# Low parts of the weights formed on GpSimd in a two-layer diffusion backbone

## The chip, the cores and the metric

One core of a Trainium2 chip runs the whole program in one launch. The metric is the time of one execution on the device, in microseconds (us); smaller is better. The engines are named as in the rows of the profile: PE is TensorE (matmuls; PEld is its weight load), DVE is VectorE, ACT is ScalarE, POOL is GpSimd, SP is SyncE, whose queue issues nearly all transfers.

## What is computed

Two layers over 2048 latent tokens and 256 context tokens of width 1024. The even layer is a Conformer convolution (31 taps) beside a Fourier mixing, the odd layer a short gated convolution beside windowed attention. Cut to its frame:

```
def _even_mix(h, w_in, a_conv_w, a_conv_b, a_ln_g, a_ln_b, a_pw_w, a_pw_b, b_fw, w_out):
    a_val, a_glu, a_gate, b_val, b_gate = _split(h @ w_in, ...)
    u = a_val * jax.nn.sigmoid(a_glu)
    u = jax.nn.silu(_layernorm(_dwconv(u, a_conv_w) + a_conv_b, a_ln_g, a_ln_b))
    y_a = (u @ a_pw_w + a_pw_b) * jax.nn.silu(a_gate)
    y_b = _fourier_mix(b_val, b_fw) * jax.nn.silu(b_gate)
    return jnp.concatenate([y_a, y_b], axis=-1) @ w_out

# reference(), per layer
x_new = x + gt * _even_mix(_pre(x, e_norm[i], sh, sc), *args)
...
x_new = x + gt * _odd_out(cb, cc, cx, cg, att, ag, o_c_conv_w[i], o_w_out[i])
return _rmsnorm(x, final_norm)
```

All of it is in float32.

## The kernel before

A product in float32 is made of three products of a shorter format, fp32r. Each operand is split into a high part, the value rounded to fp32r, and a low part, the value less its high part, rounded too; `gemm` (lines 117 to 124) multiplies high by high (L122), high weight by low activation (L123) and low weight by high activation (L124). `split` (lines 92 to 95) forms both parts: a copy on ScalarE writes the high part (L94), a subtraction on VectorE the low part (L95).

Tokens lie along the free dimension in chunks: four of 512 latent tokens (0 to 3) and one of 256 context tokens (4). The weights come as blocks of 128 output channels. `wblock` loads a block of 1024x128 in two halves; `wload` (lines 102 to 108) does one half: a transfer on SyncE's queue into a staging tile `wst` of 128x512 (three buffers), then `split` into the tiles `wh` and `wl` (three buffers of a whole block each). The pointwise weights of the convolution go the same way under the names `pwst`, `pwh` and `pwl`, from `conv0`. There are 148 blocks and so 296 halves, and 20 halves of pointwise weights. Activations, attention probabilities and FFT intermediates go through `split` too; those calls are others than that of `wload`.

The gemms are the main line, stage by stage: `in0` (input projection of the even layer) for chunks 0, 1 and 4, `in0` for chunks 2 and 3, `wout0` (its output projection) for chunks 4 and 0, then 1, `in1` (input projection of the odd layer) for 4, 0 and 1, `wout0` for 2 and 3, `in1` for 2 and 3, `wout1` for all. A group of two or three blocks is loaded, then used for each chunk in turn. The gemms fill three PSUM buffers (`pmm`), and VectorE and ScalarE evict them.

Beside it runs a second line, `mixers` and then `attention`, woven in by `merge` with a ratio for each stage. `mixers` is: `taps` for chunks 0 and 1, `conv0(0)`, `taps` for 4, `conv0(4)`, then the four FFT groups with the modulation sums of `mod_rows` between them, then `conv0(1)`, `taps` for 2 and 3, `conv0(2)`, `conv0(3)`. A tap (L419) is one multiply-add over half a chunk or a whole one on VectorE, whose two tensor inputs (the gated signal or its differences, and the running sum) lie in SBUF; the first tap of a channel group (L454) has one tensor input. `conv0` is the layer norm, SiLU and pointwise product of the convolution. The buffers of taps and `conv0` and those of the FFT lie in the same place, one after the other; attention's come after them there.

The order of the instructions on each engine is not written out. A planner takes instructions as they become ready in its own model of the chip, by priority: the code order sets it, `high_priority` shifts it (taps are put back by 100), and it hands out the buffers. Each engine then works its list in order and waits by semaphores where an input is not there. On GpSimd that list holds 28 small memsets of tile edges, the memset of one 128x512 tile done twice at the start, and 44 issues of transfers of the DFT tables (L661), three buffers deep; the transfers of all else are on SyncE's list.

Of the kernel before, what the change touches and what calls it, by code (L numbers as in the profile page):

```python
# [9 lines left out]
F32 = mybir.dt.float32  # L10
# [3 lines left out]
ALU = mybir.AluOpType  # L14
# [60 lines left out]
class Kernel:  # L75
# [26 lines left out]
    def wload(self, src, w, k, kt=KT):  # L102

        pre = "w" if kt == KT else "pw"
        pool, bufs = (self.wp, 3) if kt == KT else (self.vp, 1)
        st = self.tl(pool, [P, 4, P], F32, pre + "st", bufs=bufs)
        self.nc.sync.dma_start(st, src[:, k : k + 4])
        self.split(st, w[0][:, k : k + 4], w[1][:, k : k + 4])

    def wblock(self, src, kt=KT):  # L110

# [1270 lines left out]
```

## Time and profile before

| | before |
|---|---|
| median of three runs | 1931.48 us |
| lowest and highest | 1931.21 and 1932.12 us |
| the profiled execution | 1931.29 us |
| its span (first to last instruction) | 1929.5 us |
| PE busy | 1850.1 us, 96% |
| DVE busy | 1471.3 us, 76% |
| ACT busy | 917.6 us, 48% |
| POOL busy | 35.6 us, 2% |

Busy times are of one profiled execution. Matmuls overlap, and their ends are modelled, so a busy PE is not PE at its peak. Instructions of one engine overlap a little as well: their durations add up to more than the distance of their starts. An L with a number is a line of the kernel before. A releaser is what ended an engine's idle time, inferred from semaphores.

### The profile page before, as it was taken

How to read it: one execution, taken by the hardware profiler on the slowest of the kernel's cores; microseconds unless marked ns; L12 is line 12 of the kernel's file. 1: busy time of each engine (PE TensorE's matmuls, PEld its weight loads, DVE VectorE, ACT ScalarE, POOL GpSimd, SP SyncE). 2: the span in 40 equal slices, each digit the busy share in tenths (PEclk: the TensorE clock that was granted, in tenths of full speed). 3: DMA queues.
4: the chain of work that ended last, by engine and by line, in shares of the span. 5: the costliest groups of instructions: out<-in, count | busy, mean ns of one | idle time of the engine just before them, and what ended most of it. 6: DMA issues, size and time to landing. Idle time of an engine off the chain costs nothing.

```text
span 1929.5 us, 26744 instructions
## 1 busy us (share of the span) xinstructions
PE 1850.1 (96%) x9140; PEld 1498.5 (78%) x9140; DVE 1471.3 (76%) x3234; ACT 917.6 (48%) x1630; POOL 35.6 (2%) x78
## 2 busy tenths in 40 slices
PE   6899999989999999999999999999999999999997
PEld 2688878867777887888877877777787777888887
DVE  4799999879986989999644567688745556577866
ACT  5732242523223534422332666565665655576543
POOL 0000000011011000000000000000000000000000
PEclk9999999999999999999999999999999999999998
DMA  8433242778677487774135246567633232354754
GB/s 308 139 112 114 88 134 89 239 227 257 231 228 208 152 281 238 217 202 144 59 120 161 92 140 212 159 191 200 167 112 110 83 98 74 96 178 146 227 179 159
DMA packets 216600, 316.87 MB, mean 164 GB/s; under 512 B 22928, under 2 KB 102288, under 8 KB 215440
## 3 DMA queue, kind: packets, MB, share of 16 engines
q1 hardware_dynamic: 204496, 299.96, 49.6%
q0 software_dynamic: 11968, 15.21, 3.2%
q8 instruction: 72, 1.18, 0.3%
q14 instruction: 64, 0.52, 0.1%
HBM read 240.90 MB, written 74.19 MB: 163 GB/s over the span
## 4 chain that ended last, share of the span: by engine, by line
PE 68%; DVE 11%; issue 10%; DMA 8%; ACT 2%; SPq 0%; POOL 0%; DVEq 0%; POOLq 0%; ACTq 0%
PE mm L123 18%; PE mm L124 18%; PE mm L122 18%; DVE z L419 5%; PE pv L930 4%; PE pt L995 4%; PE s L930 4%; DMA et<-in_e_tab 2%; DMA xk<-gbd 1%; DMA act<-in_e_w_mod 1%; DMA yd<-pev 1%; DVE wl L95 1%; DMA wst<-in_e_w_out 1%; DMA pwst<-in_e_a_pw_w 1%; ACT S L980 1%
## 5 line engine op out<-in xcount | busy, mean ns | idle before, releaser
L122 PE MATMUL mm<-act,wh 128*128 128x512 f32 (+1 forms) x2288 | 861.7, 378 | 11.8 <-ACT act L211 10.0
L123 PE MATMUL mm<-act,wh 128*128 128x512 f32 (+1 forms) x2288 | 863.8, 378 | 0.3 <-DVE act L95 0.2
L124 PE MATMUL mm<-act,wl 128*128 128x512 f32 (+1 forms) x2288 | 860.6, 377 | 0.9 <-DVE wl L95 0.9
L122 PEld LDWEIGHTS mm<-act,wh 128*128 128x128 f32 x2288 | 431.9, 189 | 84.4 <-ACT act L211 11.5
L123 PEld LDWEIGHTS mm<-act,wh 128*128 128x128 f32 x2288 | 432.3, 189 | 71.2 <-issue 2.6
L124 PEld LDWEIGHTS mm<-act,wl 128*128 128x128 f32 x2288 | 432.4, 189 | 69.5 <-issue 2.4
L94 ACT CAST wh<-wst 128x512 fp32r<-128x512 f32 x296 | 176.3, 620 | 283.9 <-PE mm L123 217.7
L95 DVE TENSOR_TENSOR wl<-wst,wh 128x512 fp32r<-128x512 f32 x296 | 197.7, 686 | 55.2 <-ACT wh L94 53.2
L419 DVE SCALAR_TENSOR_TENSOR z<-d,e_a_conv_w,z 128x504 f32<-128x504 f32 (+2 forms) x372 | 206.4, 611 | 0.2
L95 DVE TENSOR_TENSOR pl<-pt,ph 128x512 fp32r<-128x512 f32 x156 | 102.0, 686 | 54.0 <-ACT ph L94 53.1
L94 ACT CAST ph<-pt 128x512 fp32r<-128x512 f32 x156 | 85.4, 590 | 99.9 <-PE pt L995 92.2
L980 ACT ACTIVATE S<-S,nb 128x640 f32<-128x640 f32 (+1 forms) x128 | 103.0, 806 | 57.2 <-DVE nb L976 57.1
L995 PE MATMUL pt<-ident,S 128*128 128x128 f32 x624 | 121.6, 274 | 2.3 <-ACT S L987 1.4
L995 PEld LDWEIGHTS pt<-ident,S 128*128 128x128 f32 x624 | 80.2, 140 | 40.6 <-ACT S L987 15.1
L419 DVE SCALAR_TENSOR_TENSOR z<-ut,ws,z 128x504 f32<-128x504 f32 (+2 forms) x180 | 101.6, 610 | 0.1
L987 ACT ACTIVATE S<-S,sm 128x640 f32<-128x640 f32 (+1 forms) x128 | 94.0, 806 | 9.9 <-DVE sm L985 9.8
L960 DVE CUSTOM_DVE_ANT_0 S<-s,mask 128x384 f32<-128x384 f32 (+1 forms) x128 | 68.6, 536 | 16.4 <-PE s L930 9.9
L211 ACT ACTIVATE act<-nu,mod 128x512 fp32r<-128x512 f32 (+1 forms) x80 | 52.5, 678 | 42.2 <-DVE nu L210 41.9
L930 PE MATMUL s<-kw,qs 128*128 128x384 f32 (+1 forms) x256 | 67.3, 343 | 1.6 <-DMA kw<-kd 1.3
L212 DVE SCALAR_TENSOR_TENSOR act<-nu,mod,act 128x512 fp32r<-128x512 f32 (+1 forms) x80 | 54.7, 694 | 6.5 <-ACT act L211 6.1
L969 DVE TENSOR_SCALAR_CACHE_REDUCE S<-s 128x256 f32<-128x256 f32 x128 | 53.5, 419 | 6.0 <-PE s L930 5.5
L930 PEld LDWEIGHTS s<-kw,qs 128*128 128x128 f32 x256 | 44.0, 188 | 15.8 <-DVE mx L960 5.3
(252 smaller groups left out, 2034.7 us busy)
## 6 DMA issues: line engine op xcount, KB each, us to landing
wst<-in_o_w_in SPq DMA_DIRECT2D x104, 256.0 KB, 3.2
wst<-in_e_w_in SPq DMA_DIRECT2D x80, 256.0 KB, 3.3
wst<-in_o_w_out SPq DMA_DIRECT2D x64, 256.0 KB, 3.3
mw<-in_o_w_mod SPq DMA_DIRECT2D x48, 256.0 KB, 3.6
wst<-in_e_w_out SPq DMA_DIRECT2D x48, 256.0 KB, 3.8
et<-in_e_tab POOLq DMA_DIRECT2D x28, 384.0 KB, 4.4
kw<-kd SPq DMA_DIRECT2D x28, 384.0 KB, 3.5
act<-in_e_w_mod SPq DMA_DIRECT2D x32, 256.0 KB, 5.4
```

The source lines that it names most:

```text
L94: nc.scalar.copy(hi, src)
L95: nc.vector.tensor_tensor(lo, src, hi.bitcast(F32), ALU.subtract)
L122: mm(ps, hi[:, k, :], act.hi[k], start=k == 0, stop=False)
L123: mm(ps, hi[:, k, :], act.lo[k], start=False, stop=False)
L124: mm(ps, lo[:, k, :], act.hi[k], start=False, stop=k == kt - 1)
L212: nc.vector.scalar_tensor_tensor(act.lo[k], u, sh[:, k, v : v + 1], act.hi[k].bitcast(F32), ALU.add, ALU.subtract)
L419: nc.vector.scalar_tensor_tensor(*a)
L930: nc.tensor.matmul(*a, **kw)
L960: nc.vector.tensor_tensor_reduce(s[:, :nw], ps[:, :nw], self.mask[:, m0 : m0 + nw], op0=ALU.add, op1=ALU.max, scale=1.0, scalar=-3.0e38, a ...
L980: nc.scalar.activation(S[h], S[h], AF.Exp, bias=nb4[:, h : h + 1], scale=SM_SCALE, accum_out=sm[:, h : h + 1],)
L987: nc.scalar.activation(S[h], S[h], AF.Copy, scale=sm[:, h : h + 1])
L995: nc.tensor.transpose(pt[:, h * P : (h + 1) * P], S[h][:, i * P : (i + 1) * P], self.ident)
```

## The change

`wload` no longer calls `split`. It writes the high part with the same copy on ScalarE and forms the low part with the same subtraction, issued on GpSimd. All other calls of `split` stay on VectorE.

```diff
--- before.py
+++ after.py
@@ -105,7 +105,9 @@
         pool, bufs = (self.wp, 3) if kt == KT else (self.vp, 1)
         st = self.tl(pool, [P, 4, P], F32, pre + "st", bufs=bufs)
         self.nc.sync.dma_start(st, src[:, k : k + 4])
-        self.split(st, w[0][:, k : k + 4], w[1][:, k : k + 4])
+        hi, lo = (x[:, k : k + 4] for x in w)
+        self.nc.scalar.copy(hi, st)
+        self.nc.gpsimd.tensor_tensor(lo, st, hi.bitcast(F32), ALU.subtract)
 
     def wblock(self, src, kt=KT):
 
```

## Rows read from the trace of the kernel before

**Rows 1.** The page, part 1: busy us, share of the span, instructions.

```profile
PE 1850.1 (96%) x9140; PEld 1498.5 (78%) x9140; DVE 1471.3 (76%) x3234; ACT 917.6 (48%) x1630; POOL 35.6 (2%) x78
```

**Rows 2.** By stage: length; busy of PE, PEld, DVE, ACT, POOL; clock; DMA.

```profile
0.00:96.00 96.00, 71.58 (x313) 44.18 (x314) 60.61 (x120) 62.02 (x96) 1.35 (x8) 0.96 0.66 224
96.00:365.00 269.00, 263.30 (x1356) 222.62 (x1357) 259.00 (x532) 93.53 (x157) 1.11 (x10) 1.00 0.39 121
365.00:620.00 255.00, 234.11 (x1194) 193.16 (x1192) 209.09 (x507) 71.18 (x138) 31.85 (x47) 0.98 0.77 234
620.00:936.00 316.00, 309.18 (x1446) 255.71 (x1447) 303.38 (x509) 126.84 (x215) 0.25 (x3) 0.99 0.63 193
936.00:1320.00 384.00, 373.89 (x1754) 295.98 (x1752) 242.05 (x573) 202.23 (x360) 0.69 (x7) 1.00 0.48 150
```

**Rows 3.** What PE waited for, whole span: us in total, times, longest.

```profile
PE aux L638 <- DMA et<-in_e_tab: 10.8, 15, 2.4
...
PE aux L630 <- DVE fG L618: 5.8, 1, 5.8
...
PE mm L124 <- DVE wl L95: 0.9, 3, 0.4
```

**Rows 4.** Chain that ended last, by line, 96 to 365, 620 to 936.

```profile
by line: PE mm L124 21.7%; PE mm L122 21.5%; PE mm L123 21.4%; DVE z L419 15.9%; DMA pwst<-in_e_a_pw_w 3.2%; DMA wst<-in_e_w_in 2.5%; issue 1.8%; DVE wl L95 1.3%; DVE lt L95 1.0%; DVE pwl L95 1.0%; ACT z L533 0.8%; DVE pev L553 0.7%; ACT pw
...
by line: PE mm L123 19.2%; PE mm L122 19.1%; PE mm L124 19.0%; DVE z L419 18.5%; DMA wst<-in_e_w_out 4.1%; issue 3.0%; DVE wl L95 2.3%; DMA xk<-gbd 1.4%; DMA ga<-gad 1.3%; DMA xk<-yd 1.3%; ACT wh L94 1.0%; DVE act L95 1.0%; PE aux L194 1.0%
```

**Rows 5.** Groups of DVE, 96 to 365: count, busy us, mean ns, idle before.

```profile
L419 DVE SCALAR_TENSOR_TENSOR z<-d,e_a_conv_w,z 128x504 f32<-128x504 f32 x124 | 83.4, 735 | 0.1
...
L95 DVE TENSOR_TENSOR wl<-wst,wh 128x512 fp32r<-128x512 f32 x38 | 25.8, 684 | 2.7 <-ACT wh L94 2.7
...
L95 DVE TENSOR_TENSOR pwl<-pwst,pwh 128x512 fp32r<-128x512 f32 x8 | 5.5, 691 | 2.5 <-ACT pwh L94 2.5
```

**Rows 6.** Timeline of DVE at 223.5: start us, us, instruction.

```profile
223.50 0.68 DVE L95 TENSOR_TENSOR wl<-wst,wh 128x512 fp32r<-128x512 f32 x1
224.11 0.73 DVE L419 SCALAR_TENSOR_TENSOR z<-d,e_a_conv_w,z 128x504 f32<-128x504 f32 x1
```

**Rows 7.** Groups of POOL, whole span.

```profile
L661 POOL DMA_DIRECT2D et<-in_e_tab x44 | 31.6, 719 | 269.6 <-PE aux L638 179.7 <-DMA bvd<-ev 77.1 <-DMA et<-in_e_tab 9.0
...
L234 POOL MEMSET ev<- 128x512 f32 x2 | 1.0, 525 | 0.3 <-POOLq L1377 0.3
L438 POOL MEMSET ut<- 128x15 f32 x8 | 0.9, 112 | 123.0 <-DVE z L419 114.9 <-DVE lt L493 8.1
```

**Rows 8.** Timeline at 154, DVE and POOL.

```profile
154.27 0.54 DVE L454 TENSOR_SCALAR z<-ut,ws,e_a_conv_b 128x504 f32<-128x504 f32 x1
154.46 0.39 POOL L436 MEMSET ut<- 128x15 f32 x1 [43.12 <-DMA wst<-in_e_w_in]
```

**Rows 9.** Timeline at 197, DVE and POOL.

```profile
196.87 1.39 DVE L419 SCALAR_TENSOR_TENSOR z<-ut,ws,z 128x504 f32<-128x504 f32 x2
...
197.71 0.11 POOL L436 MEMSET ut<- 128x15 f32 x1 [42.85 <-DVE z L419]
```

**Rows 10.** Instructions with wl by stage: length; PE, PEld, DVE busy us (count).

```profile
365.00:620.00 255.00, 98.37 (x248) 47.24 (x248) 20.05 (x30) 0.98 0.77 234
620.00:936.00 316.00, 170.25 (x458) 86.53 (x458) 42.52 (x64) 0.99 0.63 193
```

**Rows 11.** What POOL waited for, 365 to 620.

```profile
POOL et L661 <- PE aux L638: 179.7, 21, 54.4
```

**Rows 12.** What the queue of SP waited for, 560 to 700.

```profile
SPq L107 <- DVE wl L95: 8.1, 8, 3.7
SPq L711 <- DVE lt L95: 5.1, 1, 5.1
```

**Rows 13.** Line 393 (evictions of in0's last kind), 600 to 700.

```profile
L393 ACT ACTIVATE ev<-mm x8: 581/598/602, 615.9 to 662.7; 128x512 f32<-128x512 f32 x8
```

**Rows 14.** Timeline of SP at 1047.

```profile
1047.89 0.47 SPq L315 DMA_DIRECT2D kw<-kd  x1
```

## The prediction

> **What bounds the kernel now.** I read the page first, then one table of engine time by stage, then what TensorE waited for, then the chain of waits in the two stages in which VectorE is full, and last the rows of GpSimd. The page [rows 1] shows TensorE busy for 1850.1 of 1929.5 us and GpSimd for 35.6. So at most 79.4 us can be had by feeding TensorE better. The table by stage [rows 2] says where VectorE matters: from 96 to 365 us it is busy for 259.0 of 269.0 us, from 620 to 936 for 303.4 of 316.0, while TensorE has 5.7 and 6.8 us idle there. From 365 to 620 VectorE has 45.9 us idle, from 936 to 1320 142.0. The list of TensorE's waits [rows 3] is to be read for what is not in it: the instruction that the change moves, the forming of wl, is waited for 3 times, 0.9 us in all. Larger are its waits for the DFT tables (10.8 us in 15 waits) and for one of the FFT's additions on VectorE (5.8 us). The chain of waits [rows 4] gives VectorE's convolution taps (L419) 15.9% of the stage 96 to 365 and 18.5% of the stage 620 to 936, and wl 1.3% and 2.3%: 0.013 x 269 + 0.023 x 316 = 10.8 us. So TensorE bounds, and VectorE is level with it in two stages: its taps fill every gap, and what follows them (the layer norm of the convolution, then the FFT in the place of its buffers) starts when they end.
>
> **What is removed.** All 296 wl and the 20 pwl leave VectorE; line 108 is their only source. One takes 684 ns [rows 5], and the next instruction starts 0.61 us after it (223.50 to 224.11) [rows 6], so a stage loses 0.61 us of VectorE for each: 46 of them from 96 to 365 (38 + 8) [rows 5] are 28.1 us. Of that little was on the path: TensorE's own waits for wl, 0.9 us [rows 3], are the direct gain, and I take 1 us.
>
> **What is added, on GpSimd.** No row of before shows an elementwise operation with two inputs on this engine. Its nearest row is the memset of the same 128x512 tile, one pass of writes: 525 ns [rows 7]. Lower bound of the price: VectorE's 0.68 us [rows 5]. Upper bound: three such passes one behind the other, two reads and a write, 1.58 us. I take two passes, 1.05 us, since that row is of the same engine, and the write can run beside the reads. 296 + 20 of them are 332 us of GpSimd, 17% of the span, so the engine is not filled.
>
> **Do the two engines get in each other's way?** Two pairs of rows bear on it. The memset of 15 columns takes 112 ns as a rule [rows 7], and it does so beside a tap [rows 9]. But at 154.46 it took 0.39 us, beside the one kind of tap instruction with a single tensor input (L454, 154.27 to 154.81), and ended with it, 0.04 us later [rows 8]. So there are VectorE instructions that hold GpSimd off until they are done. Whether a GpSimd instruction that reads two tiles holds off a tap, which also reads two tiles of SBUF, no row shows. The bounds: each wl on GpSimd gives VectorE back 0.61 us and blocks it for nothing (net -0.61), or it gives back 0.61 and blocks VectorE for its whole duration (net 1.58 - 0.61 = +0.97 at the dear price). I take a full block at 1.05 us, net +0.44 us, because the only instructions that show an interaction show a wait to the end of the other, and because a tap and the moved instruction are alike in reading two tiles of SBUF, where the memset reads none.
>
> The Trainium skill, "SBUF — State Buffer", section "SBUF: two separate sides", has a rule that speaks against this change: VectorE and GpSimd share a pair of ports as an exclusive lock, a VectorE operation with two SBUF inputs collides only with a GpSimd operation that reads SBUF, and the one that starts first holds the pair for its whole instruction. The two pairs of memset rows (which only write) agree with that as far as they go; by the rule the net is +0.44 us, and without the lock -0.61. The Trainium skill, "GPSIMD Engine Reference", section "Elementwise — side-by-side cycle accounting", gives two-input fp32 work on GpSimd 1.96 times VectorE's duration; as an estimate that is 1.34 us here, a net of +0.73, and the sum below would be about 1959 us.
>
> **The sum by stage.** 0 to 96 us: 8 wl, in a stage that leaves VectorE 35.4 us idle [rows 2]; nothing. 96 to 365: 46 x 0.44 = 20.2 us more of VectorE; its 10.0 us of idle time take the first part, and 10.2 us come out at the end, where the last of conv0(4) makes room for the FFT's tiles. 365 to 620: 31 x 0.44 = 13.6 us (30 wl [rows 10] and one pwl) fit into 45.9 us of idle time; nothing more, but nothing comes back either, since the FFT's chain is one of transfers and waits. Its end gates conv0(1), and conv0(1) gates wout0: the queue of SyncE stands for 5.1 us at the first loads of wout0's activations, behind conv0(1)'s last low part [rows 12]. The last eviction of in0 is at 662.7 us [rows 13], so TensorE has no other matmuls left there, and I take the 10.2 us as idle time of TensorE. 620 to 936: 68 x 0.44 = 29.9 us (64 wl [rows 10] and 4 pwl), 12.6 of them into idle time, 17.3 us pushed on. They delay the last taps, and the first loads of attention, which follow them at 1047.89 us [rows 14]. Taken at nothing: matmuls of in1 stand ready for TensorE, and VectorE has 142.0 us of idle time in the next stage [rows 2]; if that cover is gone it costs up to 17.3. After 936: VectorE is busy for 63% of the stage up to 1320, and less is asked of it; nothing.
>
> **Queues.** The cast on ScalarE, the staging load and its slot stay, but the slot is now released by GpSimd: SyncE's queue waited 8.1 us for wl in 8 waits between 560 and 700 us [rows 12], with the loads of activations and the stores behind it. A wl that comes 0.4 to 0.5 us later adds about 4 us to these waits, half of it seen by TensorE: +2 us (0 to 11, the whole of wl's share of the chain again). On GpSimd's own queue the wl now stand among the 44 issues of DFT tables, 0.72 us each [rows 7]. An issue behind a wl is late by up to 1.05 us; GpSimd is busy with wl for 30 x 1.05 = 32 of 255 us there, so some 5 or 6 of 44 issues meet one, half of it each: +2 us on the 15 waits for tables (0 to 16, if all 15 meet one). The other way round, a wl behind an issue that waits for TensorE is a rival below.
>
> Sum: -1 + 10.2 + 2 + 2 = +13.2 us. The profiled execution took 1931.3 us (span 1929.5), 0.2 below the median of 1931.48; 1931.3 + 13.2 + 0.2 = 1944.7, so **1945 us**.
>
> **Rivals.**
> A, absorbed. VectorE's taps are filler; if the 10.2 us at 365 are taken back inside the 20.9 us that TensorE idles from 365 to 620 [rows 2], only the queues are left: +0 to +4 us, 1933 us. For it: TensorE has enough matmuls of in0 through the whole of that stage. Against it: the loads that wait for conv0(1) [rows 12].
> B, faster: the two engines do not collide, or only briefly. It decides at a block of under 0.61 us for each wl. Then VectorE is 28.1 us ahead at 365, the FFT starts sooner, and TensorE's waits for VectorE fall: 5.8 us at the FFT's additions, 0.9 at wl [rows 3], and about 5.1 at wout0's loads [rows 12]: 11.8 us at most. I take 8: 1923 us. For it: memsets ran undisturbed beside taps [rows 9]. Against it: the one that did not [rows 8].
> C, much slower: GpSimd's queue is one line. The issues of DFT tables stood there for 179.7 us in 21 waits for TensorE [rows 11]. A wl behind such an issue is late although its inputs are ready, and matmuls of in0 stop for it. At 1 us for each of the 21, with the forecast's 13.2 and the 17.3 us of the stage up to 936 also coming through: 1931.5 + 13.2 + 21 + 17.3 = 1983 us; one of the two alone gives 1962 to 1966. It decides where the planned order, which places a wl where its inputs are due, is off by more than the time by which wl are early.
>
> **How the numbers follow.** Forecast (1936 to 1958) 0.42, A 0.20, B 0.20, C 0.18. Within 0.2%, about what a measurement of this kernel can tell from no change, is 1927.6 to 1935.4. B lies below it, of A nearly all is within it, forecast and C are above. Faster 0.22, same 0.19, slower 0.59. The range takes in A, most of B and the two single cases of C, and the dear price of the forecast (46 x 0.97 - 10.0 = 34.6 in place of 10.2, 1969 us): 1920 to 1972.
>
> **What would show it.** Right: a wl on GpSimd of 1.0 to 1.3 us; taps beside one that read 1 us longer or start later; VectorE's busy time down by less than the 191 us that 316 x 0.61 gives, or up; the FFT's first table later than now; a wait of TensorE at 660 to 700 us. Taps of unchanged 735 ns [rows 5] beside wl would make B right and the forecast wrong. An unchanged end of conv0(4) with the same time would say A; matmuls of in0 that wait for wl on GpSimd, between 365 and 620 us, would say C. The step that I trust least is the 10.2 us that goes from VectorE's overrun to TensorE.

## The result: 6.5% slower, and the profile after

The changed kernel takes 2057.8 us (median; 2055.3 to 2059.1) where the kernel before takes 1931.6 beside it: a ratio of 1.0646, with a 95% interval of 1.0629 to 1.0664. The change costs 126 us. The forecast was 1945 us, with a range of 1920 to 1972: the sign was right and the time lies 86 us above the range.

The rows of the changed kernel have its own line numbers, two higher behind `wload`: L421 is the tap, L110 GpSimd's low part. Each experiment's rows likewise have those of its kernel. The first part of the page (busy us, share of the span, instructions) answers [rows 1]; under it, from its second part, TensorE's busy tenths in 40 slices of the span:

```profile
PE 1884.1 (92%) x9140; PEld 1516.2 (74%) x9140; DVE 1458.2 (71%) x2918; ACT 922.6 (45%) x1633; POOL 529.1 (26%) x394
...
PE   7799898888989988979899999998999999999997
```

GpSimd now works for 529.1 us instead of 35.6. VectorE has 316 instructions less, but its busy time fell only from 1471.3 to 1458.2 us, by 13.1, where 316 x 0.61 would be 193. TensorE does the same 9140 matmuls in 1884.1 us instead of 1850.1. So the 123.7 us by which the span grew (2053.2 against 1929.5) are 89.7 us more of idle TensorE and 34.0 us more of TensorE at work, at a lower granted clock (0.97 in the mean, before 0.99). The digits show where: the sevens and eights lie in the first half.

The stages, cut as in [rows 2] (length; busy us and instructions of PE, PEld, DVE, ACT, POOL; granted clock; DMA):

```profile
96.00:365.00 269.00, 238.30 (x1161) 198.74 (x1160) 252.74 (x467) 79.46 (x133) 89.62 (x47) 0.95 0.31 98
365.00:620.00 255.00, 219.26 (x1103) 182.06 (x1101) 200.09 (x430) 68.23 (x126) 76.59 (x69) 0.95 0.68 208
620.00:936.00 316.00, 276.86 (x1306) 226.47 (x1307) 279.56 (x412) 118.19 (x208) 96.29 (x71) 0.94 0.62 189
936.00:1320.00 384.00, 367.14 (x1661) 292.99 (x1659) 208.68 (x428) 163.88 (x283) 85.87 (x66) 0.98 0.44 134
```

In 96 to 365 us TensorE is busy for 238.3 us where it was 263.3, at a clock of 0.95 where it was 1.00; the next two stages lose 14.9 and 32.3 us of TensorE's work. From 936 to 1320 us the loss is 6.8.

TensorE's waits (us in all, times, longest), which answer [rows 3]:

```profile
PE bg L522 <- DVE lt L518: 18.7, 2, 9.9
PE aux L196 <- DVE rb L188: 17.0, 3, 8.3
...
PE mm L126 <- POOL wl L110: 12.3, 4, 9.9
PE aux L640 <- DMA et<-in_e_tab: 9.4, 14, 1.8
...
PE aux L196 <- DVE nt L188: 7.9, 2, 4.3
PE aux L632 <- DVE fG L620: 7.8, 1, 7.8
...
PE bg L126 <- POOL pwl L110: 6.4, 8, 1.1
```

The waits for the DFT tables did not grow (9.4 us in 14, before 10.8 in 15). Much longer are the waits for VectorE's sums: lt, which the layer norm's mean needs, and rb and nt, which hold squares and their sums for the norms. In the kernel before they were:

```profile
PE aux L194 <- DVE rb L186: 3.2, 1, 3.2
...
PE bg L520 <- DVE lt L516: 1.8, 2, 1.0
```

New is a wait of 9.9 us for a low part on GpSimd. Summed over the whole list by the engine that ended the wait, TensorE waited 101.6 us for VectorE and 21.7 for GpSimd; before, 30.6 for VectorE and nothing for GpSimd. The groups of VectorE from 96 to 365 us (count, busy us, mean ns), which answer [rows 5]:

```profile
L421 DVE SCALAR_TENSOR_TENSOR z<-d,e_a_conv_w,z 128x504 f32<-128x504 f32 x124 | 87.8, 779 | 0.1
...
L456 DVE TENSOR_SCALAR z<-ut,ws,e_a_conv_b 128x504 f32<-128x504 f32 x3 | 3.5, 1183 | 0.0
```

Those of GpSimd over the whole span, which answer [rows 7]:

```profile
L110 POOL TENSOR_TENSOR wl<-wst,wh 128x512 fp32r<-128x512 f32 x296 | 465.7, 1589 | 1203.0 <-ACT wh L109 1142.8 <-DMA mw<-in_o_w_mod 23.8 <-DMA wst<-in_e_w_in 8.6
...
L110 POOL TENSOR_TENSOR pwl<-pwst,pwh 128x512 fp32r<-128x512 f32 x20 | 29.1, 1457 | 111.6 <-ACT pwh L109 108.1 <-DMA ga<-gad 3.5
```

And the view of that one tile (duration in ns: least, median, greatest):

```profile
L110 POOL TENSOR_TENSOR wl<-wst,wh x296: 1257/1302/18003, 26.3 to 2026.7; 128x512 fp32r<-128x512 f32 x148
```

The 124 taps are still 735 ns as a rule; their mean is 779 because six last 1.4 to 1.8 us. Even the operation with one tensor input (L456), 535 ns in the kernel before, has a mean of 1183. A low part on GpSimd has a mean of 1589 ns, but half of them take up to 1302, and one 18003. That one in the timeline (start us, us), which joins instructions that follow each other:

```profile
213.41 21.38 POOL L110 TENSOR_TENSOR wl<-wst,wh 128x512 fp32r<-128x512 f32 x3 [5.71 <-ACT wh L109]
```

And VectorE's timeline where it ends:

```profile
226.38 2.70 DVE L421 SCALAR_TENSOR_TENSOR z<-d,e_a_conv_w,z 128x504 f32<-128x504 f32 x4
229.00 0.69 DVE L452 TENSOR_TENSOR d<-ut 128x519 f32<-128x519 f32 x1
...
230.22 1.74 DVE L421 SCALAR_TENSOR_TENSOR z<-ut,ws,z 128x504 f32<-128x504 f32 x1
231.88 1.77 DVE L517 TENSOR_TENSOR lt<-lt,z 128x512 f32<-128x512 f32 x1
```

From 213.41 us the subtraction on GpSimd stands beside 24 taps of unchanged 0.74 us (the DVE rows before 229), and gets through only at 230, beside the next row's first tap, which lasts 1.74 us. The GpSimd row runs over three low parts in a row, to 234.8; the two behind the first take 1.72 and 1.66 us and lengthen the next VectorE instructions to 1.77. So there are two effects: GpSimd can be **held off** by VectorE, and when it gets in it **blocks** VectorE for about 1 us.

The issues of DFT tables on GpSimd (first and last start), before and after, as the view of that tile has them:

```profile
L661 POOL DMA_DIRECT2D et<-in_e_tab x44: 716/716/832, 370.8 to 594.2; - x44
...
L663 POOL DMA_DIRECT2D et<-in_e_tab x44: 713/713/859, 401.5 to 650.4; - x44
```

And the last evictions of the first projections, which answer [rows 13]:

```profile
L395 ACT ACTIVATE ev<-mm x8: 580/598/601, 672.0 to 724.7; 128x512 f32<-128x512 f32 x8
```

The FFT's first table is issued at 401.5 us instead of 370.8. The last of those evictions starts at 724.7 us instead of 662.7. GpSimd's issues waited 88.1 us for TensorE over the whole span, less than the 179.7 of [rows 11].

### The profile page after: what moved, and what is told of

Same layout as the page of the kernel before. It is cut to its first block, busy times and chain, and to the rows that moved or that the text cites. A ratio compares the mean times of both kernels' runs of the same rounds, so it can differ in the third digit from the quotient of the medians.

```text
span 2053.2 us, 26873 instructions
## 1 busy us (share of the span) xinstructions
PE 1884.1 (92%) x9140; PEld 1516.2 (74%) x9140; DVE 1458.2 (71%) x2918; ACT 922.6 (45%) x1633; POOL 529.1 (26%) x394
## 5 line engine op out<-in xcount | busy, mean ns | idle before, releaser
L126 PE MATMUL mm<-act,wl 128*128 128x512 f32 (+1 forms) x2288 | 872.3, 382 | 12.4 <-POOL wl L110 12.3
L110 POOL TENSOR_TENSOR wl<-wst,wh 128x512 fp32r<-128x512 f32 x296 | 465.7, 1589 | 1203.0 <-ACT wh L109 1142.8
L124 PEld LDWEIGHTS mm<-act,wh 128*128 128x128 f32 x2288 | 437.0, 191 | 93.8 <-ACT act L213 10.5
L126 PEld LDWEIGHTS mm<-act,wl 128*128 128x128 f32 x2288 | 437.7, 191 | 85.0 <-POOL wl L110 14.5
L125 PEld LDWEIGHTS mm<-act,wh 128*128 128x128 f32 x2288 | 437.7, 191 | 79.2 <-DVE act L95 5.7
L421 DVE SCALAR_TENSOR_TENSOR z<-d,e_a_conv_w,z 128x504 f32<-128x504 f32 (+2 forms) x372 | 236.7, 693 | 0.2
L421 DVE SCALAR_TENSOR_TENSOR z<-ut,ws,z 128x504 f32<-128x504 f32 (+2 forms) x180 | 128.1, 747 | 0.7
L188 DVE TENSOR_TENSOR rb<-rb,nt 128x512 f32<-128x512 f32 (+1 forms) x70 | 56.5, 808 | 27.0 <-ACT nt L187 26.6
L214 DVE SCALAR_TENSOR_TENSOR act<-nu,mod,act 128x512 fp32r<-128x512 f32 (+1 forms) x80 | 61.1, 774 | 8.4 <-ACT act L213 7.9
L866 DVE TENSOR_TENSOR m<-mm,ev 128x512 f32<-128x512 f32 x16 | 11.0, 690 | 77.8 <-PE mm L126 74.6
```

The costliest lines, as they stand in the source:

```text
L110: self.nc.gpsimd.tensor_tensor(lo, st, hi.bitcast(F32), ALU.subtract)
L124: mm(ps, hi[:, k, :], act.hi[k], start=k == 0, stop=False)
L125: mm(ps, hi[:, k, :], act.lo[k], start=False, stop=False)
L126: mm(ps, lo[:, k, :], act.hi[k], start=False, stop=k == kt - 1)
L421: nc.vector.scalar_tensor_tensor(*a)
```

## The experiments

Theory 1: GpSimd's operation on two SBUF tiles and VectorE's operations on SBUF tiles exclude each other, and this costs the time. Theory 2: the change made the planner lay another order of instructions, and the order is worse. Theory 3: only GpSimd's longer time and the low parts' lateness cost. Theory 4: any pass of GpSimd over SBUF costs VectorE its time.

### Is it GpSimd's reading? (e8, e9, e12)

> The changed kernel, in which GpSimd sets each low part to zero instead of forming it: the same tiles are written by the same engine and read by TensorE, in nearly the instruction order of the change, but GpSimd reads nothing. Theory 1 (GpSimd's reads of two tiles beside VectorE's reads of two tiles): near the kernel before, 1925 to 1945 us. Theory 2 (the changed order of instructions costs): stays at 2040 to 2070 us. Theory 4 (any pass of GpSimd over SBUF costs VectorE its time, here 0.53 us instead of 1.26): 1970 to 2000 us.

```
-        self.nc.gpsimd.tensor_tensor(lo, st, hi.bitcast(F32), ALU.subtract)
+        self.nc.gpsimd.memset(lo.bitcast(F32), 0.0)
```

Measured: 1920.7 us, 0.9943 of the kernel before (0.9920 to 0.9965), 4 us below the range of theory 1. Of TensorE's 9140 matmuls in the order of the trace, a comparison line by line finds 192 that stand elsewhere than in the changed kernel; for the kernel before it finds 737. So with nearly the order of the change, with GpSimd writing the same tiles and TensorE waiting for them, the loss is gone, and 10 us beside it. Theories 2 and 4 fall. The run takes away two things at once, GpSimd's reading and more than half of its time (0.53 us instead of 1.26); the next two take them apart. A memset on GpSimd added to the kernel before (e5) gave no time: with its tile the others no longer fitted in SBUF (11 kb a partition needed, 10.3 left). The write-only kernel also gives each VectorE instruction of the change its undisturbed twin. Its page:

```profile
PE 1847.5 (96%) x9140; PEld 1499.1 (78%) x9140; DVE 1292.8 (68%) x2918; ACT 921.6 (48%) x1633; POOL 191.3 (10%) x394
```

An addition of two SBUF tiles (L188) among its groups:

```profile
L188 DVE TENSOR_TENSOR rb<-rb,nt 128x512 f32<-128x512 f32 x49 | 33.7, 688 | 12.2 <-ACT nt L187 11.7
```

The same group in the changed kernel, and one that reads PSUM, the masked scores:

```profile
L962 DVE CUSTOM_DVE_ANT_0 S<-s,mask 128x384 f32<-128x384 f32 x112 | 61.9, 553 | 12.1 <-PE s L932 9.2 <-PE pt L997 1.7
...
L188 DVE TENSOR_TENSOR rb<-rb,nt 128x512 f32<-128x512 f32 x49 | 45.1, 920 | 21.0 <-ACT nt L187 20.7
```

VectorE's busy time is 1292.8 us here and 1458.2 there, for the same 2918 instructions: 165 us are waiting for GpSimd, written down as work. Taken instruction by instruction (each one's duration less the median of its form here) it is 164.9 us, and 187 instructions are more than 0.3 us longer, by 0.89 us on average. By stretch of the span, all instructions together grew by 33.5 us from 96 to 400 us (35 of the 187), by 18.6 up to 655 (22), by 49.3 up to 1000 (54) by 58.2 behind it (70), and by 5.2 before 96 us (6). The additions at L188 go from 688 to 920 ns. The masked scores, which read PSUM, keep their 553 ns.

> The changed kernel in which GpSimd writes half of the staged weight as the low part (a one-input operation of 128x512) instead of the difference: nearly the same order of instructions, the same tiles written and waited for, but one tile read instead of two. In the second microkernel three one-input operations lengthened a row of 36 taps by 0.67 us, three two-input ones by 3.0 us. Theory 1 (two reads are what blocks): 1925 to 1960 us. Rival (any read of GpSimd's blocks VectorE): 2020 to 2060 us.

```
-        self.nc.gpsimd.tensor_tensor(lo, st, hi.bitcast(F32), ALU.subtract)
+        self.nc.gpsimd.tensor_scalar(lo, st, 0.5, None, ALU.mult)
```

Measured: 1985.3 us, 1.0285 (1.0259 to 1.0311), between what the two said. One read costs too, if less: VectorE's instructions are 37.8 us longer in all, 90 of them by 0.37 us on average, though GpSimd itself is slower at it (mean 1718 ns, instead of 1589). Neither "only two reads" nor "any read as much" holds, and GpSimd's longer time by itself does not make the whole loss.

> The changed kernel in which GpSimd forms the low parts of only half the columns of each staged half block (128x256) and sets the other half to zero. Theory 1b (the length of GpSimd's two-input operation is what VectorE waits): the operation is some 0.65 us, a blocked operation waits some 0.4 us instead of 1.0; about 40% of the 126 us stay: 1965 to 2000 us. Rival (each collision costs a fixed time, whatever its length): 2040 to 2060 us.

```
-        self.nc.gpsimd.tensor_tensor(lo, st, hi.bitcast(F32), ALU.subtract)
+        self.nc.gpsimd.tensor_tensor(lo[:, 0:2], st[:, 0:2], hi[:, 0:2].bitcast(F32), ALU.subtract)
+        self.nc.gpsimd.memset(lo[:, 2:4].bitcast(F32), 0.0)
```

Measured: 1981.3 us, 1.0240 (1.0208 to 1.0271): 50 of 126 us, the 40% that theory 1 named. The half subtraction has a median of 742 ns, and a blocked VectorE instruction waits 0.46 us (121 of them). The price goes with the length of GpSimd's operation.

### What is freeing VectorE worth, and does TensorE's wait for the low part matter? (e1, e2)

> The kernel before, in which no low part of a weight is formed on any engine, and the third product of each group reads the high part again; TensorE's work is the same. What freeing VectorE can bring at most. Theory 1 and theory 3: VectorE gives up 0.61 us at 316 places, of which only the stretch 96 to 365 us is set by VectorE and TensorE waits there 10 us in all: 1915 to 1932 us. If VectorE's load were the price elsewhere too (316 x 0.61 = 193 us at the utmost), under 1900 us. Theory 2 (the planner's order of the instructions is what costs): another order, so 1960 us or more is possible.

```
-        return tuple(self.tl(pool, [P, kt, P], F32R, pre + x, bufs=bufs) for x in "hl")
+        return tuple(self.tl(pool, [P, kt, P], F32R, pre + x, bufs=bufs) for x in "h") * 2
...
-        self.split(st, w[0][:, k : k + 4], w[1][:, k : k + 4])
+        self.nc.scalar.copy(w[0][:, k : k + 4], st)
...
-            mm(ps, lo[:, k, :], act.hi[k], start=False, stop=k == kt - 1)
+            mm(ps, hi[:, k, :], act.hi[k], start=False, stop=k == kt - 1)
```

Measured: 1929.5 us, 0.9989 (0.9971 to 1.0007). Taking 180 us off VectorE (1291.5 us busy) for nothing in return does not move the kernel by what a measurement can tell; the kernel with memsets alone gained 0.6%. So there was next to nothing to win (0.1 to 0.6%), and no version of this idea was found that beats the kernel before.

> The changed kernel, in which GpSimd forms every low part as there, but the third product reads the high part, so that TensorE waits for no low part. Theory 1 (contention for the read of two SBUF tiles): the held-off low parts still keep their staging tile, and the blocked taps and adds still take 1.7 us, so most of the 126 us stays: 2010 to 2045 us. Theory 3 (only the low part's lateness at TensorE costs): 1930 to 1945 us.

```
-            mm(ps, lo[:, k, :], act.hi[k], start=False, stop=k == kt - 1)
+            mm(ps, hi[:, k, :], act.hi[k], start=False, stop=k == kt - 1)
```

Measured: 2066.3 us, 1.0695 (1.0664 to 1.0726): nothing of the loss goes, though TensorE waits for no low part any more; theory 1, too, had expected less, 2045 us at most. Theory 3 falls in its plain form. What is left of it is that a late low part holds its staging tile, and so the next load; that is the same in this run. The time of that wait turns up elsewhere: before the layer norm's mean (L522) TensorE stands for 20.0 us for lt and 16.5 us at its own issue.

### In which stage? (e3, e4, e10, e11)

> The change only behind the convolution of chunk 3 (some 960 us into the span): before that VectorE forms the low parts as in the kernel before, behind it GpSimd does. Theory 1: behind that point VectorE has no rows of taps and TensorE sets the time, so within 0.5% of before, 1925 to 1941 us. Theory 3 (GpSimd's longer time alone costs): half of the weights move, so some 60 us of the 126 stay, 1980 to 2000 us.

> The complement: GpSimd forms the low parts up to the end of the convolution of chunk 3, VectorE behind it. Theory 1: nearly the whole loss, 2030 to 2065 us. Theory 3: the other half of the loss, 1980 to 2000 us.

> GpSimd forms the low parts only up to the end of the first input projection (chunks 0, 1 and 4; to about 365 us in the kernel before), VectorE behind it. In that stretch VectorE is busy nearly throughout, most of it with operations on two SBUF tiles. Theory 1: about 46 to 50 low parts at up to 1.06 us minus the 0.61 us taken off VectorE, and the delays that follow at TensorE: 1945 to 1975 us. Theory 2 (order, all over): 1932 us.

> GpSimd forms the low parts only from the end of the first input projection to the end of the convolution of chunk 3; VectorE before and behind it. Theory 1: the rest of the early loss of 114 us, together with the run in which GpSimd is used only up to the first projection's end about 114 us over the kernel before: 1995 to 2030 us. What my prediction had for this stretch (pushed on, but at nothing): 1925 to 1940 us.

The four differ only in how the flag begins and where it turns: at the first place below, at the second, or at both. This is the run of the middle:

```
+        self.late_on = False
...
-        self.nc.gpsimd.tensor_tensor(lo, st, hi.bitcast(F32), ALU.subtract)
+        eng = self.nc.gpsimd if self.late_on else self.nc.vector
+        eng.tensor_tensor(lo, st, hi.bitcast(F32), ALU.subtract)
...
                 self.merge(in0, bg, R[0], OFF[0])
+                self.late_on = True
...
                 self.drain(bg, lambda: {2, 3} <= self.ya_done)
+                self.late_on = False
```

Measured: first projection only 1967.0 us (1.0181, 1.0156 to 1.0205), middle only 2008.8 (1.0390, 1.0365 to 1.0415), late only 1941.9 (1.0053, 1.0033 to 1.0072), first and middle 2044.9 (1.0589, 1.0565 to 1.0613). Over the kernel before these are 35.7, 77.4 and 11.2 us, 124 together, and 114 for the first two: the stages add up. The late part, with 132 of the 316 low parts, costs 11 us where theory 3 had some 60 (and theory 1 at most 10). The flag's last turn comes later than the expectation said, at 1119 us of the span with GpSimd late and 1232 with GpSimd early. What TensorE waits for in 96 to 400 us when only this first stage has GpSimd's low parts:

```profile
PE mm L128 <- POOL wl L112: 11.0, 2, 10.4
PE aux L198 <- DVE nt L190: 8.7, 2, 6.8
PE bg L524 <- DVE lt L520: 8.4, 1, 8.4
PE bg L128 <- POOL pwl L112: 4.8, 6, 1.1
```

TensorE idles 34 of these 304 us: 16 for low parts (10.4 of them one that was held off), 18 for VectorE's sums. Now the same stage, from 96 us to the FFT's first table. The kernel before (one stretch a line):

```profile
96.00:370.80 274.80, 269.10 (x1382) 227.48 (x1383) 264.05 (x541) 95.60 (x160) 1.11 (x10) 1.00 0.39 124
```

The changed kernel:

```profile
96.00:401.50 305.50, 270.21 (x1345) 226.90 (x1344) 273.20 (x492) 94.91 (x159) 102.50 (x57) 0.95 0.35 108
```

The kernel whose GpSimd only writes:

```profile
96.00:360.00 264.00, 261.35 (x1351) 222.40 (x1351) 237.08 (x490) 95.05 (x158) 21.24 (x51) 1.00 0.38 124
```

It lasts 274.8, 305.5 and 264.0 us. TensorE is idle for 5.7, 35.3 and 2.7 us of it. VectorE is busy 9 us longer with the change than before, and idle for 32.3 us instead of 10.8. So VectorE has not become the bound by its busy time: the engines wait for one another.

### How do they exclude each other? (m1 to m4)

Four small kernels run only rows of VectorE instructions of 128x512 and GpSimd operations beside them.

> A kernel that does none of the reference's work: eleven stretches, in each 28 operations of VectorE in a row (56 in the one of half width) of 128x512, and beside them three operations of GpSimd, which begin after VectorE's second. Theory 1 (GpSimd's two-input operation is held off while VectorE runs operations with two SBUF inputs back to back, and when it gets in, holds VectorE for about 1.06 us): alone 1.25 to 1.3 us each; beside taps that read two SBUF tiles 3 to 18 us for one, or an end only when the row of taps is over; the same beside a plain two-input subtraction; beside one-input operations and beside taps of which one or both inputs are in PSUM 1.3 us, and VectorE unchanged; with a one-column operation after every fourth tap at most 5 us (four taps of 0.74 us and its own time); GpSimd's one-input operation and its memset get through beside taps in under 1 us. Theory 3 (only GpSimd's own time is longer, no contention): 1.3 us in every stretch, and each tap 0.74 us.

> A kernel that does none of the reference's work: ten stretches, each bound to begin when both engines are done with the one before. In each, VectorE runs 36 operations of one kind in a row (72 of half width, none in the stretch called alone), and GpSimd begins three operations of 128x512 behind VectorE's third. Theory 1 (a two-input operation of GpSimd is held off while VectorE runs operations on two SBUF tiles back to back): alone 1.26 us each; beside taps on two SBUF tiles, beside the plain two-input operation and beside taps of half width GpSimd's first ends only when the row is over, 20 us or more, and VectorE's operations keep 0.74 and 0.68 us; beside one-input operations and taps on PSUM 1.26 to 1.4 us each, VectorE unchanged; with a one-column one-input operation after every fourth tap each GpSimd operation ends within 5 us and one tap beside it takes 1.7 us. In the first trial of this kind a one-input operation of GpSimd took 1.8 to 2.1 us beside taps, so it is expected to be held off as well; the memset, which reads nothing, 0.5 us. Rival (whichever engine begins first holds the port for its operation, in turns): GpSimd waits at most one tap, so 2.0 us each and one tap of 1.7 us for each, beside every kind of two-input row.

> A kernel that does none of the reference's work: as the second of these, ten stretches with 36 operations of VectorE in a row (72 of half width) and three operations of GpSimd that begin behind the third, but VectorE's operations add to two tiles in turn, so that each may begin before the one before has ended (in the changed kernel 193 of its 504-wide taps begin 0.65 or 0.66 us after the one before, which lasts 0.74; in the second kernel of this kind each waited for the one before, and began 0.79 us after it). Theory 1a (only such overlapping rows hold GpSimd off): beside taps and beside the plain two-input operation in turns GpSimd's first two-input operation ends only when the row is over, some 24 us, and VectorE keeps 0.66 and 0.60 us for each; with a one-column operation after every fourth tap, with two taps in a row on one tile, and with a read of PSUM in every fourth place each GpSimd operation ends in under 5 us and costs VectorE about 1.0 us; its one-input operation and memset end in under 2 us. Rival (by turns, as in the second kernel of this kind): 1.7 to 2.0 us for each GpSimd operation in every stretch.

> A kernel that does none of the reference's work: twelve stretches of 39 operations of VectorE, most of them taps that add to two tiles in turn, and in each one two-input subtraction of GpSimd that comes only some 3.5 us into the row, behind six memsets of GpSimd's own (and none to four memsets of one column, which shift it within a tap). In the kernels of this kind so far GpSimd's operation came right behind a small operation of VectorE, and was never held off; in the changed kernel the subtraction that took 18.0 us came 7 us into a row of 24 more taps. Theory 1a (one that comes into the middle of a row of overlapping taps is held off to its end or to VectorE's first wait): 15 us or more beside the taps and the plain two-input operation at some or all of the five shifts; 2 us or less beside taps that each wait for the one before, and at most 5 us where every eighth operation reads PSUM; a one-column memset after every fourth tap does not help. Rival (by turns, wherever it comes): 1.7 to 2.0 us in every stretch; the 18 us would then need another cause.

In the first one the instructions of different stretches were mixed by the scheduler, so its stretches can't be told apart; the other three bind them. Operations of GpSimd in the second, as groups (count, busy us, mean ns):

```profile
L40 POOL TENSOR_TENSOR lo_taps<-st,hi 128x512 f32<-128x512 f32 x3 | 5.0, 1653 | 0.2
...
L40 POOL TENSOR_TENSOR lo_one<-st,hi 128x512 f32<-128x512 f32 x3 | 4.0, 1322 | 0.2
...
L40 POOL TENSOR_TENSOR lo_psum<-st,hi 128x512 f32<-128x512 f32 x3 | 3.8, 1262 | 0.2
```

And in the third:

```profile
L41 POOL TENSOR_TENSOR lo_turns<-st,hi 128x512 f32<-128x512 f32 x3 | 4.8, 1610 | 0.2
...
L41 POOL TENSOR_TENSOR lo_alone<-st,hi 128x512 f32<-128x512 f32 x3 | 3.8, 1261 | 0.2
L47 POOL MEMSET lo_pset<- 128x512 f32 x3 | 1.6, 524 | 0.2
```

Alone a low part takes 1261 ns, and beside taps on PSUM 1262, with nothing lost on either side. Beside taps on SBUF it is 1610 to 1653: it waits for the tap that runs, at most, and the next tap waits 1.0 us for it (1.75 instead of 0.75 us). "Held off", which theories 1 and 1a expected, did not come in the second and third kernel; "by turns", the rival's, did. Not expected: a row of one-input operations from SBUF to SBUF (lo_one) is blocked too, 1.37 us for 0.49. The memset takes 524 ns and costs VectorE nothing.

In the fourth, GpSimd's operation comes 3.5 us into a row, behind six memsets of its own and none to four more of one column, which shift it within a tap (timeline: start us, us):

```profile
11.12 1.47 POOL L41 TENSOR_TENSOR lo_t<-st,hi 128x512 f32<-128x512 f32 x1
...
38.82 1.32 POOL L41 TENSOR_TENSOR lo_t6b<-st,hi 128x512 f32<-128x512 f32 x1
...
66.52 19.05 POOL L41 TENSOR_TENSOR lo_t6c<-st,hi 128x512 f32<-128x512 f32 x1
...
94.08 18.89 POOL L41 TENSOR_TENSOR lo_t6d<-st,hi 128x512 f32<-128x512 f32 x1
...
121.66 18.74 POOL L41 TENSOR_TENSOR lo_t6e<-st,hi 128x512 f32<-128x512 f32 x1
...
229.65 17.37 POOL L41 TENSOR_TENSOR lo_plain<-st,hi 128x512 f32<-128x512 f32 x1
...
254.28 1.26 POOL L41 TENSOR_TENSOR lo_chain<-st,hi 128x512 f32<-128x512 f32 x1
```

The first two got in at the next tap (1.47 and 1.32 us, the second column); the other three were held off, 18.7 to 19.1 us, by taps that kept their 0.75 us. So both happen, beside the same row of taps. Of the ten rows of taps in turn, with 504 columns and 512, and with or without an eighth operation on PSUM or a one-column memset, five got in and five did not; the two-input row without taps held it off for 17.4 us. All six hold-offs ended at the last VectorE instruction of the row, which for once waited for the one before it (it began 0.72 to 0.78 us behind one that lasted 0.68 to 0.75). Where each tap waits for the one before it (lo_chain) GpSimd got in at once: there a tap begins 0.79 us after the last, in the other rows 0.66 us after it, before its 0.75 us are over.

What decides between the two stays open. In these rows of taps those with none or one of GpSimd's one-column memsets got in and those with two to four did not, and the memsets also set the place in the tap: of the five rows shown, 0.39 and 0.55 us into it got in, 0.04, 0.20 and 0.36 did not. The place alone is not the rule in the changed kernel, where a low part that came 0.04 us into a tap of such a row got in at the next one:

```profile
688.99 1.85 POOL L110 TENSOR_TENSOR wl<-wst,wh 128x512 fp32r<-128x512 f32 x1 [1.77 <-ACT wh L109]
```

One that came at 252.51 us, 0.01 us into a tap, took 8.78. The two variants that were to show whether a read of PSUM or a one-column memset on VectorE lets GpSimd in (lo_evict, lo_blank) have no memset of GpSimd's ahead, as lo_t, which got in without either, and show nothing.

### Can the collisions be made cheaper? (e6, e7)

> The changed kernel with a one-column memset on VectorE behind every fourth convolution tap, so that GpSimd finds a break in a row of taps. The longest low part falls from 18 us to under 5 us. Theory 1a (what costs is that low parts are held off for 5 to 18 us): most of the loss goes, 1950 to 1990 us. Theory 1b (what costs is that each low part, when it gets in, holds VectorE's two-input operation for about 1.06 us): the loss stays, 2035 to 2070 us.

```
+        gap = self.tl(self.vp, [P, 1], F32, "gap", bufs=1)
+        taps = [0]
...
                 nc.vector.scalar_tensor_tensor(*a)
+                taps[0] += 1
+                if taps[0] % 4 == 0:
+                    nc.vector.memset(gap, 0.0)
```

Measured: 2053.1 us, 1.0640 (1.0610 to 1.0671). The longest low part takes 19.3 us, in the same row of taps. But the planner did not leave the memsets behind their taps: it placed 138 of them in VectorE's list, and none between 193.6 and 233.5 us, where that row stands. So the run shows neither whether a one-column memset is a break nor which of its two theories holds.

> The changed kernel with GpSimd's subtraction in four pieces of 128x128, each 0.45 us when alone. Theory 1b: GpSimd's time in all grows from 1.26 to about 1.65 us a low part, each block of a tap falls from 1.06 to about 0.35 us, but there are up to four of them: 2050 to 2110 us. Rival (a block under the length of VectorE's own operation is hidden): 1990 to 2030 us.

```
-        self.nc.gpsimd.tensor_tensor(lo, st, hi.bitcast(F32), ALU.subtract)
+        for q in range(4):
+            self.nc.gpsimd.tensor_tensor(lo[:, q], st[:, q], hi[:, q].bitcast(F32), ALU.subtract)
```

Measured: 2051.5 us, 1.0626 (1.0595 to 1.0657), in the range of theory 1b. VectorE's instructions are longer by 97.0 us in all instead of 164.9, but the loss is the same: GpSimd's own time grew to 798.3 us, and one piece was still held off for 16.5 us.

### How does VectorE's lateness become idle time of TensorE? (e13, e14)

In the change the planner had put the layer norm's mean matmuls (L522, before L520) earlier in TensorE's list: the first by some 40 matmuls, the second by 79. It seems to have laid the order for a VectorE with less to do: the first began at 248.8 us in the kernel before, at 237.8 with GpSimd only writing, and at 261.9 with the change.

> The changed kernel with one number altered, the urgency of the layer norm's mean matmul (L522, from 1000 to 0), so that it stands later in TensorE's fixed order: at rows 1118, 1528, 2872, 4284 and 4475 instead of 1003, 1355, 2695, 3903 and 4388. In the changed kernel TensorE stood 9.0 and 10.1 us before two of these matmuls, for VectorE's sums. Theory 5 (the order is laid for a VectorE that is not blocked, and TensorE, which cannot pass a matmul whose input is late, turns VectorE's lateness into idle time): part of these 19 us comes back, 2030 to 2050 us. Rival (lateness moves on to whatever needs the convolution's result next): 2053 to 2075 us.

> The kernel before with the same one number altered: the mean's matmuls at rows 1118, 1528, 2874, 4286 and 4477 instead of 1045, 1434, 2702, 4091 and 4391. It shows what the altered number does by itself. Theory 5: in the kernel before TensorE waits only 1.0 and 2.3 us at the first of them, so there is nothing to win and the convolution's result comes later: 1930 to 1950 us.

```
-TOT = [2000, 300, 1000, 300, 300, 2000, 1000]
+TOT = [2000, 300, 0, 300, 300, 2000, 1000]
```

Measured: the changed kernel 2068.5 us (1.0715, 1.0680 to 1.0750), 11 us more than without it; the kernel before 1958.2 (1.0132, 1.0104 to 1.0160), 26 us more, 8 beyond what was expected of it. The rival was right: a later place for these matmuls wins nothing, the lateness moves on. That the altered number costs less beside the change than without it fits theory 5, and is no proof of it.

## Why the prediction was wrong

**What bounds.** That TensorE bounds, and that little was to be won by VectorE, held: 0.1% without any low part formed (e1).

**Price of a low part.** Taken at 1.05 us, with bounds of 0.68 and 1.58. Measured 1.26 us alone, 1.30 in the median: within the bounds, and above the value taken. The Trainium skill, "GPSIMD Engine Reference", section "Elementwise — side-by-side cycle accounting", has the ratio of 1.96 that gave the estimate of 1.34, which is nearer; here the ratio is 1.84 (1.26 over 0.684).

**The block.** "A full block" was the right mechanism. A VectorE instruction that is caught waits 1.0 us, and the memset, which reads nothing, does not disturb. The Trainium skill, "SBUF — State Buffer", section "SBUF: two separate sides", says that a VectorE operation with two SBUF inputs collides only with a GpSimd operation that reads SBUF; the taps on SBUF and on PSUM and the write-only kernel agree. But the term was counted once for each of 316 low parts, and only 187 instructions were caught. In the first stage the sum had 46 x 1.05 - 46 x 0.61 = +20.2 us of VectorE, and the trace, up to 400 us, has 33.5 - 28.1 = +5.4; by busy time up to the FFT's first table it is 273.2 - 264.1 = +9.1. This term was two to four times too large; on the count of VectorE's time alone the forecast should have been nearer to no change.

**From VectorE's time to the kernel's time: the step that failed.** The sum subtracted a stage's idle time from a stage's overrun of VectorE (20.2 - 10.0 = 10.2 us to the FFT's start), took the overrun of 365 to 620 at nothing since 45.9 us of idle time were there, and the 17.3 us of 620 to 936 at nothing since matmuls stood ready (17.3 at most if they did not). It was the step I said I trusted least, and it was wrong in kind, not only in size. What counts is how late one result is where TensorE's next matmul in order needs it; idle time elsewhere in the stage does not cover that. The waits for lt reached 9.9 us, those for rb 8.3, and the one behind the hold-off of 18 us 9.9. The FFT's start moved by 30.7 us instead of 10.2, on an overrun of VectorE of only 5 to 9 us, and the first stage cost 35.7 us (e10). The idle time lay in that stage itself (35.3 us before the first table, before the change 5.7), and not behind in0's last eviction, where TensorE waited 4.7 us. The middle, taken at nothing, cost 77.4 (e11), and the late part, also at nothing, 11.2 (e3). The half-length subtraction shows it best: with it VectorE is busy for 1352.7 us, 119 less than before the change, and the kernel is 50 us slower. What stays open is the share of each: the loss is 0.8 us for each microsecond that VectorE's instructions grew in the changed kernel (136 over 164.9, counted from the write-only kernel: 126 + 10), 1.1 in the half-length kernel (60 over 56.0), 1.3 with the four pieces (129 over 97.0) and 1.7 in the one-input kernel (63 over 37.8), so the blocks alone do not set it. TensorE's waits grew by 71 us where a result of VectorE ended them and by 22 where one of GpSimd did. But with no low part to wait for (e2) they lay at VectorE's results instead; no run separates the two.

**The clock.** No term stood for it. Three long stops of TensorE that were looked at (at 222, 338 and 981 us) are followed by 10 us at a granted clock of 0.86, 0.83 and 0.78. Around the stop at 222 us (stretches of 10 us; PE busy and count, ..., clock, DMA):

```profile
212.00:222.00 10.00, 9.55 (x57) 8.17 (x55) 10.00 (x17) 2.32 (x5) 8.59 (x1) 1.00 0.05 17
222.00:231.50 9.50, 0.03 (x1) 0.03 (x1) 9.50 (x14) 0.00 (x0) 9.50 (x2) 0.61 0.00 0
231.50:241.50 10.00, 10.00 (x38) 8.17 (x39) 9.82 (x11) 2.20 (x4) 5.11 (x5) 0.86 0.61 184
241.50:251.50 10.00, 10.00 (x56) 8.71 (x56) 10.00 (x16) 1.19 (x2) 0.00 (x0) 1.00 0.15 54
```

Before the stop the clock is at its upper level, 2.4 GHz (1.00); in the stop and behind it the mean is 0.61 and 0.86, as parts of the time are at 1.2 GHz, and TensorE, busy for all of the 10.0 us behind it, does 38 matmuls instead of 56. Over the span TensorE's busy time is 34.0 us longer for the same matmuls, more than a quarter of the loss; that all of it is the clock is not shown by a run.

**Held off.** The prediction read from [rows 8] that one VectorE instruction can hold GpSimd off to its end. That a row of them can, one beginning before the other has ended, was not thought of. The runs show both turns and hold-offs of 18 to 19 us. The rule of the Trainium skill, "SBUF — State Buffer", section "SBUF: two separate sides", that the one which starts first keeps the ports for its whole instruction, tells of turns alone; here the measurement decides.

**Queues.** The 2 us for DFT tables behind low parts did not come: TensorE's wait for tables fell a little. SyncE's queue waits longer for low parts at a load, in the whole span before and after (the kind of wait of [rows 12]):

```profile
SPq L107 <- DVE wl L95: 278.2, 219, 17.5
...
SPq L107 <- POOL wl L110: 411.3, 196, 17.4
```

The prediction had about 4 us more of these waits between 560 and 700 us; over the whole span they grew by 133. The run without a reader (e2) shows that TensorE's own wait for low parts is not what costs, and what the later loads cost no run shows.

**The rivals.** A (absorbed) is refuted by the time, B (a block of under 0.61 us) by the taps of 1.75 us. C gave the nearest time, 1983 us at most, by the wrong mechanism: GpSimd's issues of tables waited less for TensorE than before, not more, the low part for which TensorE waited 9.9 us stood behind taps, not behind an issue, and between 401 and 680 us no matmul waited for a low part. Its 17.3 us of the stage up to 936 did come through, and more.

**What was to show it.** Right, as listed: low parts of 1.3 us, taps a microsecond longer, VectorE's busy time down by far less than the sum of 316 x 0.61 (which is 193 us, not 191), a later first table. The sign that it should have named is in the list of waits: TensorE waiting for VectorE's sums, lt 18.7 us instead of 1.8.

## What to carry to other kernels

Before moving a two-input SBUF operation to GpSimd, look at what VectorE runs at the same time: rows of operations on SBUF tiles collide with it, operations on PSUM and GpSimd's memsets do not. Price a collision by the instruction that it hits and by who waits for that one in order, not by a stage's sum of busy time; a kernel whose TensorE is 96% busy has little idle time to cover it, and here it also lost clock behind each long stop that was looked at. Ask first what the relief is worth: a run without the moved work at all (here 0.1%) is the cheapest experiment.

## What the runs showed of the hardware

- GpSimd's subtraction of 128x512 took 1.26 us alone and beside VectorE's taps on PSUM, 1.3 to 1.7 us beside taps on SBUF when it took turns, and up to 19.1 us in other rows of taps that began 0.66 us apart and lasted 0.75 us each. In the fourth small kernel the six that were held off got in where a VectorE instruction for once began after the end of the one before.
- A tap on SBUF caught by it lasted 1.75 us instead of 0.75, a one-input operation from SBUF to SBUF 1.37 instead of 0.49; a one-input GpSimd operation lengthened instructions by 0.37 us, a memset by nothing.
- The trace counts the time for which an instruction is blocked or held off as busy time: 1458.2 us of VectorE against 1292.8 for the same 2918 instructions.
